# Reading the experts' two sums from GpSimd's queue, adding them on VectorE, and building the matrix of ones ahead of the last expert block

## The chip, the cores and the metric

The kernel runs on one core of one Trainium2 chip. The metric is the device time of one execution in microseconds (us), lower is better; runs are compared by their median.

## The reference, cut to what matters

Two transformer-like blocks follow one another on 512 tokens of 1024 channels. The first ends with a mixture of experts: each token goes to 6 of 64 experts, and a shared expert takes every token.

```
out = lax.map(expert_block, (slot_tok.reshape(n_blocks, MOE_BLOCK), block_exp))
weighted = (out.reshape(n_slots, d) * slot_w[:, None]).astype(h.dtype)
routed = jnp.zeros((t + 1, d), h.dtype).at[slot_tok].add(weighted)[:t]
return (routed + swiglu(hf, s_gate, s_up, s_down)).reshape(bsz, n, d)
...
x = x + gt2 * moe_ffn(...)
return rmsnorm(x, g_final)
```

The second block begins with another norm of that result and a multiplication with `w_in_2`. So the sum over experts has to be complete before the second block can start.

## The kernel before

The experts' work is cut into blocks (`BLOCKS`), each of up to 128 token slots: one expert, or two or four side by side. For each block, `blocks` (L1643) loads the experts' weights into a ring of slots (`load_block`, SyncE's queue), gathers the tokens' rows from DRAM into one of three buffers `Xt` (`gather`, L1588, an indirect DMA on GpSimd's queue), and calls `ffn` (L1598): TensorE turns the rows (`pt_xb`), VectorE and ScalarE scale them in turns into `xTb` (L1343, L1341), TensorE multiplies with gate and up (`gub`), ScalarE and VectorE make `hb` (L1615, L1617), TensorE turns it and multiplies with the down weights (`pyb`), and VectorE scales the result into `yb` (L1631). `scatter` (L1634) then adds the rows of `yb` to one of two buffers in DRAM, `yacc[0]` and `yacc[1]`, in turns, by an indirect DMA with addition on GpSimd's queue. It runs one block late, so the rows of a block are scattered after the next block's `ffn` has been issued.

The last block is not scattered. Ahead of its `ffn` the kernel calls `sums(0)` (L1682), which reads `yacc[0]` into two ring slots with four loads of 512 KB from SyncE's queue, issues the scatter that is still pending, and calls `sums(1)` for `yacc[1]`. GpSimd adds the first sum to `ysh` (L1667), the shared expert's result, four tiles of 128 tokens. After the `ffn` comes `beyond` (L1706): a loop whose count is read at run time (experts with more tokens than planned), on all five engines; its count is zero here. Behind it the second sum is added (L1672, two tiles on VectorE, two on GpSimd), and `combine` (L1689) brings in the last block's rows by TensorE: VectorE builds a matrix of ones from the token numbers (`tfe`, L1695; `ohe`, L1698, comparisons), TensorE multiplies it with `yb` in eight products (`pce`: four token tiles by two halves of the channels), and VectorE adds each from PSUM (L1704).

```
n = nc.values_load(self.nov, min_val=0, max_val=NOV)
with tc.For_i(0, n, 1) as i:
```

The second block (`block_two`, L2237) works on the same tiles, named `x` there. ScalarE squares them (L2278), VectorE multiplies them with g_final (`times`, L2271), ScalarE squares again (L2272), a short chain on VectorE makes the norms (L2282 to L2285), the tiles are scaled (L2288, L2289) and turned by TensorE (`ptn`, L2294 to L2296), and the first products `psi` follow. Their weights are loaded by SyncE (`chunk_w`, L2082) into `wraw`, rounded by ScalarE (`whi`, L273) and completed by VectorE (`wlo`, L274).

Each engine and each DMA queue works through its instructions in a fixed order. The order is not the program's: a scheduler puts it together when the kernel is built, so instructions of two blocks can stand interleaved. No order by hand is set in this part.

Of the kernel before, what the change touches and what calls it, by code (L numbers as in the profile page):

```python
# [7 lines left out]
F32 = mybir.dt.float32  # L8
# [3 lines left out]
ALU = mybir.AluOpType  # L12
# [4 lines left out]
P = 128  # L17
# [267 lines left out]
def stage_norm_in(k, pool, ps, raw):  # L285

    nc, I, V = k.nc, k.I, k.nc.vector
    k.sc = k.pers.tile([P, 8, 32], F32, name="sc")
# [23 lines left out]
    for c in range(8):  # L312
        for i0, n in ((0, 2), (2, 4)):
# [3 lines left out]
            if i0:  # L317
                V.tensor_copy(hx(c), pt)
            else:
# [830 lines left out]
class Moe:  # L1150
# [492 lines left out]
    def blocks(self, bp, ps, hooks, span):  # L1643

        pend, Xs = self.pend, self.Xs
        for n in range(*span):
            b, rows, whos = BLOCKS[n]
            if n == len(BLOCKS) - LEAVE:
                for f in self.first:
                    self.slots.remove(f)  # L1650
            if n == len(BLOCKS) - LAST:

                last = [self.load(w[0]) for _, _, w in BLOCKS[n:]]
                for i in ((0, 1), (2,)):
                    for w in last:
                        for j in i:
                            w[1](j)
            ws = self.load_block(whos)
            self.rows_ahead(min(n + AHEAD, NFIX if span[0] == 0 else len(BLOCKS)))
            if n == len(BLOCKS) - 1:  # L1660

                s0 = self.sums(0)
                while pend:
                    self.scatter(*pend.pop(0))
                s1 = self.sums(1)
                for t in range(4):
                    self.k.nc.gpsimd.tensor_tensor(self.ysh[:, t, :], self.ysh[:, t, :], s0[t], ALU.add)  # L1667
            y = self.ffn(bp, ps, ws, Xs[n], (self.twf if n < NFIX else self.tw)[:, b:b + 1], rows, f"b{b}")
            if n == len(BLOCKS) - 1:
                self.beyond(bp, ps)  # L1670
                for t in range(4):
                    (self.k.nc.gpsimd if t > 1 else self.k.nc.vector).tensor_tensor(self.ysh[:, t, :], self.ysh[:, t, :], s1[t], ALU.add)  # L1672
                self.combine(bp, ps, y, self.tok[:, b:b + 1], rows, "e")
                break
            part = self.parts(n)
            pend.append((y, part))
            if n in hooks:
                hooks[n]()
            while len(pend) > (2 if n < 3 else 1):
                self.scatter(*pend.pop(0))  # L1680

    def sums(self, i):  # L1682

        s = [self.slot(f"sum{i}{j}").rearrange("p (t d) -> p t d", t=2) for j in range(2)]
        for t in range(4):
            self.k.nc.sync.dma_start(s[t // 2][:, t % 2, :], self.yacc[i][t * P:(t + 1) * P])
        return [s[t // 2][:, t % 2, :] for t in range(4)]

    def combine(self, pool, ps, y, tok, n, nm):  # L1689

        nc = self.k.nc
        V = nc.vector
        tf = pool.tile([P, 4], F32, tag="tf", name="tf" + nm, bufs=1)
        for t in range(4):
            V.tensor_scalar(tf[0:n, t:t + 1], tok[0:n], float(-P * t), None, ALU.add)  # L1695
        oh = pool.tile([P, 8, P], F32, tag="xT", name="oh" + nm)
        for t in range(4):
            V.tensor_scalar(oh[0:n, t, :], self.col0[0:n], tf[0:n, t:t + 1], None, ALU.is_equal)  # L1698
        for t in range(4):
            for half in range(2):  # L1700
                cs = slice(512 * half, 512 * half + 512)
                pc = ps.tile([P, 512], F32, tag=("py", "tp", "gu")[(2 * t + half) % 8 // 3], name=f"pc{nm}{t}{half}")
                nc.tensor.matmul(pc, oh[0:n, t, :], y[0:n, cs], start=True, stop=True)
                V.tensor_tensor(self.ysh[:, t, cs], self.ysh[:, t, cs], pc, ALU.add)  # L1704

    def beyond(self, bp, ps):  # L1706
        k, nc, tc = self.k, self.k.nc, self.k.tc
        V = nc.vector
        n = nc.values_load(self.nov, min_val=0, max_val=NOV)
        with tc.For_i(0, n, 1) as i:  # L1710
            sl = bp.tile([P, 1], I32, tag="sl", name="sl_o")
            sw = bp.tile([P, 1], F32, tag="sw", name="sw_o")
            V.tensor_copy(sl, self.tok[:, bass.ds(i + NB, 1)])
            V.tensor_copy(sw, self.tw[:, bass.ds(i + NB, 1)])
            v = nc.sync.value_load(self.eov[:, bass.ds(i, 1)], min_val=0, max_val=NE - 1)
            src = k.I["ew"][bass.ds(v, 1)].rearrange("a p f -> p (a f)")
            ws = []
            for q in range(3):
                t = self.slot(f"ew_o{q}")
                nc.sync.dma_start(t, src[:, 2048 * q:2048 * q + 2048])  # L1720
                ws.append(t)
            X = self.gather(sl)
            y = self.ffn(bp, ps, [ws], X, sw, P, "o")
            self.combine(bp, ps, y, sl, P, "o")

# [782 lines left out]
```

## Time and profile before

| | |
|---|---|
| median of 3 runs | 2020.23 us (2017.06 to 2023.76) |
| the profiled execution, its own time | 2015.22 us |
| its span in the profile | 2013.3 us |
| mean granted clock of TensorE | 0.968 of full speed |

The profile shows the profiled execution alone; times in it count from the start of its span. PE is TensorE's matmul, PEld its weight loads, DVE is VectorE, ACT ScalarE, POOL GpSimd, SP SyncE; a name with a q (SPq) is an engine's queue of instructions that do no arithmetic, DMA issues among them. The granted clock of a stretch is given as a share of full speed.

### The profile page before, as it was taken

How to read it: one execution, taken by the hardware profiler on the slowest of the kernel's cores; microseconds unless marked ns; L12 is line 12 of the kernel's file. 1: busy time of each engine (PE TensorE's matmuls, PEld its weight loads, DVE VectorE, ACT ScalarE, POOL GpSimd, SP SyncE). 2: the span in 40 equal slices, each digit the busy share in tenths (PEclk: the TensorE clock that was granted, in tenths of full speed). 3: DMA queues.
4: the chain of work that ended last, by engine and by line, in shares of the span. 5: the costliest groups of instructions: out<-in, count | busy, mean ns of one | idle time of the engine just before them, and what ended most of it. 6: DMA issues, size and time to landing. Idle time of an engine off the chain costs nothing.

```text
span 2013.3 us, 24229 instructions
## 1 busy us (share of the span) xinstructions
PE 1826.9 (91%) x8481; PEld 1237.6 (61%) x8481; DVE 993.3 (49%) x2220; ACT 596.5 (30%) x1124; POOL 502.1 (25%) x407
## 2 busy tenths in 40 slices
PE   5897778996879999989999987999999999999998
PEld 3686556885644333333333335888888788888886
DVE  4689955668776222262222227776423453323352
ACT  5453311213423111111111114433423344323341
POOL 1314343442422222212212225342001113101300
PEclk9998988998989999999999998999999999999999
DMA  8354353226488998999999983332323423233241
GB/s 313 118 179 161 88 163 99 80 60 214 151 299 300 355 369 346 350 398 380 367 366 370 375 321 127 111 106 79 115 89 92 143 85 105 89 94 100 79 141 42
DMA packets 135555, 393.64 MB, mean 196 GB/s; under 512 B 46899, under 2 KB 59443, under 8 KB 109064
## 3 DMA queue, kind: packets, MB, share of 16 engines
q1 hardware_dynamic: 109752, 363.66, 50.7%
q0 software_dynamic: 11856, 26.83, 5.3%
q10 hardware_dynamic: 13824, 1.58, 0.5%
q8 instruction: 68, 1.11, 0.2%
q14 instruction: 55, 0.45, 0.1%
HBM read 365.19 MB, written 38.54 MB: 201 GB/s over the span
## 4 chain that ended last, share of the span: by engine, by line
PE 69%; DVE 15%; DMA 10%; ACT 3%; issue 2%; POOL 1%; SPq 0%; another core or an unknown queue 0%; ACTq 0%; POOLq 0%; DVEq 0%
PE psi L139 12%; PE gub L139 10%; PE pof L139 9%; PE psf L139 9%; PE pyb L139 6%; DMA ewrank<-ew 6%; PE psco L139 2%; DVE cfa L746 2%; PE poo L139 2%; DVE gt L569 1%; PE pxca L139 1%; PE pt_xb L142 1%; PE pm L139 1%; PE psga L139 1%; PE psgb L139 1%
## 5 line engine op out<-in xcount | busy, mean ns | idle before, releaser
L139 PE MATMUL gub<-ewrank,xTb 128*64 128x512 f32 (+5 forms) x960 | 266.6, 596 | 1.2 <-DMA ewrank<-ew 0.6
L274 DVE TENSOR_TENSOR wlo<-wraw,whi 128x1024 fp32r<-128x1024 f32 (+1 forms) x103 | 121.7, 1182 | 137.7 <-ACT whi L273 136.9
L139 PEld LDWEIGHTS gub<-ewrank,xTb 128*64 128x64 f32 (+5 forms) x960 | 90.0, 141 | 158.3 <-issue 144.1
L273 ACT CAST whi<-wraw 128x1024 fp32r<-128x1024 f32 (+1 forms) x115 | 113.8, 989 | 226.5 <-PE psi L139 50.6
L139 PE MATMUL pyb<-ewrank,hTb 128*64 128x512 f32 (+5 forms) x440 | 152.4, 607 | 3.4 <-DMA ewrank<-ew 1.4
L139 PE MATMUL psi<-xnh,whi 128*128 128x512 f32 (+1 forms) x368 | 141.2, 385 | 0.0
L139 PE MATMUL psi<-xnl,whi 128*128 128x512 f32 (+1 forms) x368 | 140.9, 383 | 0.0
L1617 DVE SCALAR_TENSOR_TENSOR hb<-gub,tw,sgb 128x256 f32<-128x256 f32 (+5 forms) x38 | 18.3, 482 | 230.3 <-ACT sgb L1615 230.3
L1639 POOL DMA_INDIRECT yacc<-yb,tok x61 | 86.1, 1411 | 158.3 <-DVE yb L1631 109.3
L1341 ACT ACTIVATE xTb<-pt_xb,B,A 128x128 f32<-128x128 f32 (+5 forms) x168 | 74.0, 445 | 173.2 <-DVE xTb L1343 171.8
L139 PE MATMUL psi<-xnh,wlo 128*128 128x512 f32 (+1 forms) x296 | 112.8, 381 | 0.0
L1593 POOL DMA_INDIRECT X<-hrow,tok x38 | 39.6, 1042 | 291.2 <-PE pt_xb L142 285.9
L1343 DVE TENSOR_SCALAR xTb<-pt_xb,A,B 128x128 f32<-128x128 f32 (+5 forms) x168 | 65.5, 392 | 88.2 <-PE pt_xb L142 51.9
L2433 POOL TENSOR_TENSOR fr<-fr 128x512 f32<-128x512 f32 x32 | 48.6, 1518 | 238.2 <-ACT fr L2432 238.2
L139 PE MATMUL psf<-xml,whi 128*128 128x512 f32 (+1 forms) x272 | 102.6, 377 | 0.2 <-DVE xml L274 0.2
L139 PE MATMUL psf<-xmh,whi 128*128 128x512 f32 (+1 forms) x272 | 102.5, 378 | 0.2 <-ACT xmh L273 0.2
L139 PE MATMUL psf<-xmh,wlo 128*128 128x512 f32 (+1 forms) x272 | 102.5, 377 | 0.0
L1631 DVE TENSOR_TENSOR yb<-pyb,gt 128x512 f32<-128x512 f32 (+5 forms) x84 | 57.9, 690 | 72.0 <-PE pyb L139 70.5
L1615 ACT ACTIVATE sgb<-gub 128x256 f32<-128x256 f32 (+5 forms) x42 | 16.0, 382 | 260.3 <-PE gub L139 260.3
L139 PEld LDWEIGHTS pyb<-ewrank,hTb 128*64 128x64 f32 (+5 forms) x440 | 46.4, 142 | 74.9 <-issue 63.7
L139 PEld LDWEIGHTS psi<-xnh,whi 128*128 128x128 f32 x368 | 69.2, 189 | 13.8 <-issue 0.2
L139 PEld LDWEIGHTS psi<-xnl,whi 128*128 128x128 f32 x368 | 69.2, 188 | 13.4
(755 smaller groups left out, 4030.1 us busy)
## 6 DMA issues: line engine op xcount, KB each, us to landing
ewrank<-ew SPq DMA_DIRECT2D x168, 1024.0 KB, 25.1
wraw<-w_in SPq DMA_DIRECT2D x59, 512.0 KB, 3.7
wraw<-ff SPq DMA_DIRECT2D x32, 512.0 KB, 3.5
wf<-ff SPq DMA_DIRECT2D x64, 256.0 KB, 2.7
wm<-w_mod SPq DMA_DIRECT2D x28, 512.0 KB, 7.8
ewfix<-ew SPq DMA_DIRECT2D x12, 1024.0 KB, 16.9
ewx<-ew SPq DMA_DIRECT2D x12, 1024.0 KB, 19.6
wm<-w_mod SPq DMA_DIRECT2D x10, 1024.0 KB, 6.2
```

What stands on the lines that cost most here:

```text
L139: return self._done(self.eng.matmul(out, lhsT, rhs, **kw), rate, rhs)
L142: return self._done(self.eng.transpose(out, in_, ident), 0.00118, ident)
L273: nc.scalar.copy(hi, raw)
L274: (eng or nc.vector).tensor_tensor(lo, raw, hi.bitcast(F32), ALU.subtract)
L569: eng.tensor_tensor(t, S[0:nq, w:32, b:w].to_broadcast([nq, n, b]), S[0:nq, b:w, 0:b].to_broadcast([nq, n, b]), ALU.mult)
L746: V.scalar_tensor_tensor(a[:, r0 * 64:r1 * 64], y[:, (r0 + o) * 64:(r1 + o) * 64], w[:, j, 15 + o:16 + o], a[:, r0 * 64:r1 * 64], ALU.mult ...
L1341: nc.scalar.activation(dst(c), pt[:, i, :], AF.Identity, scale=sa, bias=sb)
L1343: nc.vector.tensor_scalar(dst(c), pt[:, i, :], sa, sb, ALU.mult, ALU.add)
L1593: self.k.nc.gpsimd.indirect_dma_start(out=X[0:idx.shape[0]], out_offset=None, in_=self.hrow, in_offset=bass.IndirectOffsetOnAxis(ap=idx, a ...
L1631: nc.vector.tensor_tensor(y[0:n, cs], py[0:n], self.gt2[0:n, cs], ALU.mult)
L1639: self.k.nc.gpsimd.indirect_dma_start(out=self.yacc[1 - self.nsc % 2], out_offset=bass.IndirectOffsetOnAxis(ap=idx, axis=0), in_=y[a:a + n ...
L2433: nc.gpsimd.tensor_tensor(r, r, r, ALU.mult)
```

## The change

The two reads of `sums` move from SyncE's to GpSimd's queue, and each reads half of the tokens (256 rows, 1 MB) in one load. The first sum is added by VectorE and no longer by GpSimd. `combine` is split: `ones_at` builds the matrix of ones, for the last block ahead of its `ffn`, in the gather buffer `Xt[1]`, and `combine` does the eight products, now ordered so that the first two token tiles come first, half by half. The adds of the second sum (L1672) stay as they are. In `beyond`, whose loop isn't entered, the same functions are called.

```diff
                 s1 = self.sums(1)
                 for t in range(4):
-                    self.k.nc.gpsimd.tensor_tensor(self.ysh[:, t, :], self.ysh[:, t, :], s0[t], ALU.add)
+                    self.k.nc.vector.tensor_tensor(self.ysh[:, t, :], self.ysh[:, t, :], s0[t], ALU.add)
+                oh = self.ones_at(bp, self.tok[:, b:b + 1], rows, "e")
             y = self.ffn(bp, ps, ws, Xs[n], (self.twf if n < NFIX else self.tw)[:, b:b + 1], rows, f"b{b}")
...
-                self.combine(bp, ps, y, self.tok[:, b:b + 1], rows, "e")
+                self.combine(ps, y, oh, rows, "e")
                 break
...
         s = [self.slot(f"sum{i}{j}").rearrange("p (t d) -> p t d", t=2) for j in range(2)]
-        for t in range(4):
-            self.k.nc.sync.dma_start(s[t // 2][:, t % 2, :], self.yacc[i][t * P:(t + 1) * P])
+        for j in range(2):
+            self.k.nc.gpsimd.dma_start(s[j], self.yacc[i][256 * j:256 * j + 256].rearrange("(t p) d -> p t d", p=P))
         return [s[t // 2][:, t % 2, :] for t in range(4)]
 
-    def combine(self, pool, ps, y, tok, n, nm):
-
-        nc = self.k.nc
-        V = nc.vector
+    def ones_at(self, pool, tok, n, nm):
+
+        V = self.k.nc.vector
         tf = pool.tile([P, 4], F32, tag="tf", name="tf" + nm, bufs=1)
         for t in range(4):
             V.tensor_scalar(tf[0:n, t:t + 1], tok[0:n], float(-P * t), None, ALU.add)
-        oh = pool.tile([P, 8, P], F32, tag="xT", name="oh" + nm)
+
+        oh = self.Xt[1][:, 0:4 * P].rearrange("p (t a) -> p t a", t=4)
         for t in range(4):
             V.tensor_scalar(oh[0:n, t, :], self.col0[0:n], tf[0:n, t:t + 1], None, ALU.is_equal)
-        for t in range(4):
-            for half in range(2):
-                cs = slice(512 * half, 512 * half + 512)
-                pc = ps.tile([P, 512], F32, tag=("py", "tp", "gu")[(2 * t + half) % 8 // 3], name=f"pc{nm}{t}{half}")
-                nc.tensor.matmul(pc, oh[0:n, t, :], y[0:n, cs], start=True, stop=True)
-                V.tensor_tensor(self.ysh[:, t, cs], self.ysh[:, t, cs], pc, ALU.add)
+        return oh
+
+    def combine(self, ps, y, oh, n, nm):
+
+        nc = self.k.nc
+        for i, (t, half) in enumerate([(t + u, half) for t in (0, 2) for half in range(2) for u in range(2)]):
+            cs = slice(512 * half, 512 * half + 512)
+            pc = ps.tile([P, 512], F32, tag=("py", "tp", "gu")[i // 3], name=f"pc{nm}{t}{half}")
+            nc.tensor.matmul(pc, oh[0:n, t, :], y[0:n, cs], start=True, stop=True)
+            nc.vector.tensor_tensor(self.ysh[:, t, cs], self.ysh[:, t, cs], pc, ALU.add)
...
-            self.combine(bp, ps, y, sl, P, "o")
+            self.combine(ps, y, self.ones_at(bp, sl, P, "o"), P, "o")
```

## Rows read from the trace of the kernel before

**Rows 1.** The head of the page: the span and the engines' busy time.

```profile
span 2013.3 us, 24229 instructions
...
PE 1826.9 (91%) x8481; PEld 1237.6 (61%) x8481; DVE 993.3 (49%) x2220; ACT 596.5 (30%) x1124; POOL 502.1 (25%) x407
```

**Rows 2.** Table by stretches: PE, PEld, DVE, ACT, POOL busy, clock, DMA share, GB/s.

```profile
1204.00:1214.00 10.00, 5.44 (x26) 1.66 (x20) 1.87 (x3) 0.76 (x2) 9.22 (x4) 1.00 0.43 139
1214.00:1224.00 10.00, 8.83 (x16) 3.56 (x16) 8.64 (x16) 2.27 (x3) 4.79 (x5) 0.83 0.57 210
```

**Rows 3.** Timeline of POOL from 1190 us: start, duration, instruction [idle before, releaser].

```profile
1198.85 1.42 POOL L1639 DMA_INDIRECT yacc<-yb,tok  x1 [11.10 <-DVE yb L1631]
1204.78 9.26 POOL L1667 TENSOR_TENSOR h<-h,sum 128x1024 f32<-128x1024 f32 x4 [4.51 <-DMA sum<-yacc]
1218.35 4.68 POOL L1672 TENSOR_TENSOR h<-h,sum 128x1024 f32<-128x1024 f32 x2 [4.31 <-DVE h L1704]
```

**Rows 4.** SP's queue at the sums: timelines, and one of its waits (total, times, longest).

```profile
1194.63 0.81 SPq L1686 DMA_DIRECT2D sum<-yacc  x2
...
1206.31 0.80 SPq L1686 DMA_DIRECT2D sum<-yacc  x2
...
1214.28 0.80 SPq L1686 DMA_DIRECT2D sum<-yacc  x2
...
SPq L1710 <- DMA yacc<-yb,tok: 4.7, 1, 4.7
```

**Rows 5.** The chain that ended last, two of its pieces: start, us, what.

```profile
1186.33 8.25 DMA yacc<-yb,tok
...
1215.13 5.71 DMA wraw<-w_in
```

**Rows 6.** Timeline of DVE from 1190 to 1230 us.

```profile
1195.22 0.41 DVE L1343 TENSOR_SCALAR xTb<-pt_xb,A,B 128x128 f32<-128x128 f32 x1 [0.59 <-ACT xTb L1341]
1196.17 0.69 DVE L1631 TENSOR_TENSOR yb<-pyb,gt 80x512 f32<-80x512 f32 x1 [0.54 <-PE pyb L139]
...
1199.42 0.41 DVE L1343 TENSOR_SCALAR xTb<-pt_xb,A,B 128x128 f32<-128x128 f32 x1 [0.53 <-ACT xTb L1341]
1205.85 0.48 DVE L1617 SCALAR_TENSOR_TENSOR hb<-gub,tw,sgb 128x256 f32<-128x256 f32 x1 [6.03 <-ACT sgb L1615]
...
1211.09 0.69 DVE L1631 TENSOR_TENSOR yb<-pyb,gt 128x512 f32<-128x512 f32 x1 [0.21 <-PE pyb L139]
1214.37 0.34 DVE L1695 TENSOR_SCALAR tfe<-tok 128x1 f32<-128x1 int32 x4 [2.59 <-POOL h L1667]
1214.62 0.67 DVE L1698 TENSOR_SCALAR ohe<-col,tfe 128x128 f32<-128x128 f32 x3
1215.20 1.22 DVE L1672 TENSOR_TENSOR h<-h,sum 128x1024 f32<-128x1024 f32 x1
...
1221.94 2.17 DVE L274 TENSOR_TENSOR wlo<-wraw,whi 128x1024 fp32r<-128x1024 f32 x1
...
1225.83 2.35 DVE L2271 TENSOR_TENSOR h<-h,row_g_final 128x1024 f32<-128x1024 f32 x2
...
1228.17 1.21 DVE L274 TENSOR_TENSOR wlo<-wraw,whi 128x1024 fp32r<-128x1024 f32 x1
```

**Rows 7.** Timeline of TensorE's matmuls from 1185 to 1234 us.

```profile
1185.38 7.03 PE L139 MATMUL gub<-ewrank,xTb 128*80 128x512 f32 x16
...
1214.95 8.83 PE L139 MATMUL pce<-yb,ohe 128*128 128x512 f32 x16 [3.90 <-DVE ohe L1698]
1233.47 0.90 PE L142 MATMUL ptn<-cst,sums 128*128 128x128 f32 x3 [9.69 <-ACT sums L2288]
```

**Rows 8.** POOL's and SP's direct loads of 512 KB elsewhere (us to landing), POOL's time for two.

```profile
inv<-o POOLq DMA_DIRECT2D x2, 512.0 KB, 3.9
...
wraw<-w_in SPq DMA_DIRECT2D x59, 512.0 KB, 3.7
...
L580 POOL DMA_DIRECT2D inv<-o x2: 552/728/905, 269.3 to 270.4; - x2
```

## The prediction

> **What bounds the kernel now.** I read the page's head first [rows 1]: TensorE is busy for 91% of a span of 2013.3 us, so only what lets TensorE stand still can be won or lost. The change touches one seam, the end of the experts and the start of the second block, so I read only that: the table by stretches, then each queue between 1186 and 1236 us, then the chain of waits. From 1204 to 1214 us TensorE is busy for 5.44 of 10 us; in the next 10 us it is busy for 8.83, but at a mean granted clock of 0.83 [rows 2]. POOL shows why the seam starts late: its four adds of the first sum begin at 1204.78 us and take 9.26 us, to 1214.04, and the first instruction behind the loop of `beyond` (L1710) is DVE's at 1214.37, released by POOL [rows 3, 6]. Call the loop's exit E: 1214.04 now. DVE's last work ahead of it ends at 1211.78 (the last yb), so POOL holds all engines for over two microseconds. Behind E, DVE is the chain: from 1214.37 to 1225.83 it is full almost without a gap (indices, ones, two adds of sums, eight adds of products, one wlo), then come the multiplications with g_final, and TensorE's next block begins only with ptn at 1233.47, after 9.69 us of idling [rows 6, 7]. What moves ptn moves the end one for one, as TensorE is the bound behind it [rows 1].
>
> **The change part by part.** The sum is made against the profiled execution, 2015.22 us (span 2013.3); the median of the runs is 2020.23, 5.0 above it, so I add the same microseconds to the median.
>
> *The first sum's adds go from POOL to DVE.* POOL needs 9.26 / 4 = 2.3 us for one, DVE 1.22 us for the same shape [rows 3, 6]; four are 4.9 us. Without POOL's 9.26 the loop waits for the next latest: DVE's 1211.78, or SP's own wait at the loop, 4.7 us after its issue at 1206.31 to 1207.1, so about 1211.9 [rows 4, 6]. I put E at 1212.3: 1.7 us saved. The adds are not free on DVE. Their data were there at 1204.78, 10 us after the first issue at 1194.63 [rows 3, 4]. DVE idles from 1199.83 to hb at 1205.85 and from there to about 1210.2 (1211.09 less 0.21 and the 0.69 of the yb before), but only the second gap lies behind the landing, and 3.9 us of it holds three adds of four. The fourth, or one ahead of hb, costs up to 1.2 us; I take 0.6. Bounds for this term: nothing, and 3.7 us (all four ahead of hb, the first rival). Net so far: 1.1 us saved.
>
> *The reads go from SP's queue to POOL's, two of 1 MB for four of 512 KB.* POOL's direct loads of 512 KB land after 3.9 us, SP's after 3.7, and hold POOL for 0.73 us each [rows 8]; I take twice that, 1.5 us, for 1 MB, bounds 0.7 and 1.5. Ahead of the first sum POOL waits for the scatter issued at 1186.33, landed 8.25 us later, at 1194.57 [rows 5]; its two reads then occupy it to about 1197.6, and the next scatter, held until then by yb, starts at 1198.85 [rows 3]. So that scatter covers for them; without that cover they would cost up to 3 us. The second sum waits on POOL's queue for that scatter instead of on SP's; behind the waiting instruction stands only the loop, where POOL must arrive by 1212. From 1206.3 plus 2 x 1.5 us it does. Cost 0. SP loses its two reads behind the loop, which stood ahead of the weight load at 1215.13 [rows 4, 5]: 0.85 us earlier for a load that took 5.71 us. That load ends in whi and then wlo at 1221.94; DVE had other work until then, so alone it is worth nothing, but it keeps the load from becoming late when DVE's chain shrinks.
>
> *The ones are built ahead of the last ffn, in a gather buffer that the block before it read.* That removes four index adds (0.34 us) and four comparisons (0.67 for three, so 0.22 for the fourth) from DVE behind E [rows 6]. In place, 1214.37 to 1215.20 and the fourth are 1.05 us of DVE's chain; I take 1.1 saved (bounds 0.6, the advance of the first product, at E + 0.9 now and at E + 0.3 then [rows 7]; and 1.25). Their new place is DVE's idle time before hb; if that is gone they cost the same 1.25 us there.
>
> *The products' order* (two tokens' tiles, half by half) keeps the first four products on the same two tiles and the same eight PSUM tiles. Nothing waits on one tile's second half alone before all eight adds; cost 0, bounds 0.7 us either way (one add).
>
> *What else shifts.* The wlo at 1221.94 took 2.17 us, while POOL's second pair of adds ran to 1223.03; the next of its shape took 1.21 [rows 3, 6]. If the second sum lands earlier POOL's pair and the wlo no longer meet: bounds 0 and 0.96, I take 0.5. The clock: TensorE idles 3.9 us ahead of the first product, and the products take 8.83 us at 0.83 clock; at the full clock the block before did 16 in 7.03 [rows 2, 7]. With a shorter gap the clock may stay up: bounds 0 and 1.8; I take 0, since the gap remains.
>
> **Sum**: 1.1 + 1.1 + 0.5 = 2.7 us saved, 0.13%: 2015.22 becomes 2012.5, and the median 2020.23 becomes 2017.5.
>
> **A rule weighed.** POOL's scatter at 1198.85 took 1.42 us with DVE's xTb at 1199.42 beside it [rows 3, 6]; a row in which a DVE add of two SBUF operands stands beside POOL's descriptors is not there. The Trainium skill (SBUF — State Buffer, SBUF: two separate sides, the box on the "DVE blocks DMA" trap) says that a DMA issued from GpSimd waits while DVE runs a two-port instruction, and advises the SP or ACT queue, the opposite of this change; the same page (Who interferes with whom) infers that a tensor_tensor takes only the read side. By the box, the sum would lose two of DVE's adds, 2.4 us, and be 0.3; by the row it stays 2.7. I keep the row; the other case is the fifth rival.
>
> **Rivals.**
> 1. *hb waits behind all four adds.* The order on DVE is fixed before the run and not by the program: two xTb of the last block (1195.22) ran ahead of the yb of the block before it (1196.17) [rows 6]. If the adds are ordered into the gap 1199.83 to 1205.85, they wait for 1204.7 and end at 1209.6: hb is 3.7 us late, E is 1211.78 + 3.7 + 0.3 = 1215.8, 1.7 later than now; 1.1 and 0.5 come back: 2020.3. For it: the gap is the widest. Against: POOL's adds were ordered behind the scatter at 1198.85, so the order expects the sums late. Chance 0.26.
> 2. *Slower: the adds stand ahead of the last block's second pair of xTb* (the later at 1199.42). Then DVE stops until 1209.6, the pair is 10 us late, the gate products too, and E is 1211.78 + 10.3 + 0.3, about 1222.4 to 1223: 8.4 to 9 later; less 1.6, some +7.2, 2027.4. It decides from the first add that stands ahead of 1199.42 in DVE's order. Against it: in POOL's order the adds came after a scatter at 1198.85, and reads of 1 MB are ready no earlier than reads of 512 KB. Chance 0.14.
> 3. *E doesn't move*: both halves of the second sum are now issued ahead of the loop, and it waits for their landing: 1206.3 + 3.0 of issue + about 5 is 1214. Then the change does not do the first of its savings: 1.1 + 0.5, 2018.6. Chance 0.12.
> 4. *The clock stays up* and everything meets: 1.7 + 1.1 + 0.96 + 1.8 = 5.6, 2014.6. Chance 0.08.
> 5. *DVE's adds hold up POOL's reads behind E* by two adds, 2.4 us: 2017.5 + 2.4 = 2019.9. Chance 0.05; the scatter of [rows 3] speaks against it. It is what the box of the Trainium skill (SBUF — State Buffer, above) would make of this place.
>
> **How the numbers follow.** My forecast has 0.35, the rivals 0.65. A measurement of this kernel tells about 0.3%, 6 us, from no change; the three runs alone lie 6.7 us apart. All cases but the second lie within 6 us of 2020.23. The runs' spread (3 us to each side) carries a third of case 4 and a quarter or so of the forecast and of terms I have sized too small beyond 6 us: faster 0.18. Case 2, with its own spread, gives slower 0.13. The rest, 0.69, is no change. The range goes from case 4 less some of the spread, 2012, to just short of case 2, 2026; about 0.1 lies above and less below.
>
> **What would show it.** Right: no POOL adds between 1204 and E; the first instruction behind the loop near 1212.5; products starting within 0.4 us of it, no is_equal on DVE behind it; ptn 2 to 4 us earlier. The four DVE adds behind xTb at 1199.42 confirm that rival 2 is out; hb later than 1206 by up to 3.7 is rival 1. Wrong: E unmoved, or hb of the last block later than 1210, or ptn moved while the end does not.

## The result, and the profile after

The change makes the kernel slower: 2031.68 us median of 6 runs (2027.67 to 2033.42) against 2019.38 of 6 runs of the kernel before (2017.06 to 2023.76), a ratio of 1.006 with a 95% interval of 1.0048 to 1.0073. That is 12.3 us more, outside the range of 2012 to 2026. The profiled execution took 2029.28 us with a span of 2027.3, which is 14.0 above the span of before [rows 1].

In what follows the times of the seam are counted from the start of the last block's gub products (1198.21 us in the trace before, 1197.39 in the trace after), since what lies ahead of them shifts a few microseconds from run to run. "Exit" is the start of the first pce product, the first matmul behind the loop; it stands at +16.7 before and at +28.2 after.

The head of the page of the kernel after:

```profile
span 2027.3 us, 24232 instructions
...
PE 1833.0 (90%) x8481; PEld 1239.5 (61%) x8481; DVE 998.5 (49%) x2224; ACT 596.3 (29%) x1124; POOL 498.5 (25%) x407
```

The table by stretches, with the columns of [rows 2]:

```profile
1197.00:1204.00 7.00, 2.33 (x13) 0.71 (x11) 0.00 (x0) 0.00 (x0) 0.00 (x0) 0.95 0.80 330
1204.00:1214.00 10.00, 5.49 (x14) 1.44 (x16) 6.97 (x9) 1.37 (x3) 1.54 (x1) 0.52 0.27 64
1214.00:1224.00 10.00, 6.65 (x30) 2.07 (x26) 2.88 (x4) 1.74 (x3) 1.48 (x2) 1.00 0.59 212
1224.00:1234.00 10.00, 7.13 (x16) 2.96 (x16) 8.28 (x7) 1.11 (x2) 5.71 (x4) 1.00 0.29 105
1234.00:1244.00 10.00, 0.00 (x0) 0.00 (x0) 9.69 (x27) 7.48 (x14) 0.00 (x0) 0.67 0.22 70
...
1249.00:1254.00 5.00, 3.64 (x18) 3.34 (x17) 4.72 (x13) 2.10 (x6) 3.35 (x2) 0.50 0.00 0
```

Two things are new. From 1197 to 1204 us DVE, ACT and POOL do nothing at all, and TensorE is busy for 2.33 of 7 us. And TensorE has about half of its clock while it has work to do: 0.52 from 1204 to 1214, where the kernel before had 1.00 [rows 2], and 0.50 from 1249 to 1254, from 4 to 9 us behind the start of ptn. The clock of the kernel before fell around ptn too, but mostly while TensorE idled, and it was full again 3.5 us behind ptn's start (1233.47):

```profile
1224.00:1234.00 10.00, 0.53 (x3) 0.53 (x4) 9.55 (x26) 8.44 (x15) 1.12 (x1) 0.61 0.50 157
...
1237.00:1242.00 5.00, 4.54 (x37) 4.37 (x38) 4.69 (x21) 2.27 (x6) 3.46 (x2) 1.00 0.36 107
```

DVE's timeline says what everyone waits for (it answers to [rows 6]):

```profile
1193.41 0.41 DVE L1343 TENSOR_SCALAR xTb<-pt_xb,A,B 128x128 f32<-128x128 f32 x1 [0.89 <-PE pt_xb L142]
1205.01 2.36 DVE L1667 TENSOR_TENSOR h<-h,sum 128x1024 f32<-128x1024 f32 x2 [11.19 <-DMA sum<-yacc]
1207.28 0.68 DVE L1631 TENSOR_TENSOR yb<-pyb,gt 80x512 f32<-80x512 f32 x1
1207.89 0.40 DVE L1343 TENSOR_SCALAR xTb<-pt_xb,A,B 128x128 f32<-128x128 f32 x1
1208.20 0.68 DVE L1631 TENSOR_TENSOR yb<-pyb,gt 80x512 f32<-80x512 f32 x1
1209.45 2.36 DVE L1667 TENSOR_TENSOR h<-h,sum 128x1024 f32<-128x1024 f32 x2 [0.57 <-DMA sum<-yacc]
1211.73 0.41 DVE L1343 TENSOR_SCALAR xTb<-pt_xb,A,B 128x128 f32<-128x128 f32 x1
1212.66 0.41 DVE L1343 TENSOR_SCALAR xTb<-pt_xb,A,B 128x128 f32<-128x128 f32 x1 [0.53 <-ACT xTb L1341]
1217.06 0.48 DVE L1617 SCALAR_TENSOR_TENSOR hb<-gub,tw,sgb 128x256 f32<-128x256 f32 x1 [3.99 <-ACT sgb L1615]
...
1222.90 1.22 DVE L274 TENSOR_TENSOR wlo<-wraw,whi 128x1024 fp32r<-128x1024 f32 x1
1225.84 6.27 DVE L1673 TENSOR_TENSOR h<-h,sum 128x1024 f32<-128x1024 f32 x2 [1.72 <-issue]
1232.03 4.86 DVE L1709 TENSOR_TENSOR h<-h,pce 128x512 f32<-128x512 f32 x8
```

The first sum's adds (L1667) stand in DVE's order ahead of the yb of the block *before* the last one and ahead of three of the four xTb that DVE makes for the last block. They wait 11.19 us for the reads. Everything behind them waits too: hb comes at +19.7 (before: +7.6), and the late yb holds the last scatter on POOL, which answers to [rows 3]:

```profile
1194.27 1.61 POOL L1687 DMA_DIRECT2D sum<-yacc  x2 [7.34 <-DMA ewrank<-ew]
1209.17 1.54 POOL L1639 DMA_INDIRECT yacc<-yb,tok  x1 [13.29 <-DMA wraw<-w_in]
1215.99 1.48 POOL L1687 DMA_DIRECT2D sum<-yacc  x2 [5.27 <-PE gub L139]
1225.39 5.63 POOL L1673 TENSOR_TENSOR h<-h,sum 128x1024 f32<-128x1024 f32 x2 [7.93 <-issue]
```

The scatter goes out at 1209.17 instead of 1198.85 (its row names a weight load, but yb ends at 1208.88, just ahead of it, and in the run e10 below the same row names yb). It lands 5.0 us later, and the second sum, which needs its rows, is read from 1215.99, 1.8 us behind the landing (that row names gub; in e1, where gub is long over, the reads start 1.8 us behind the landing too). Both of its halves now stand ahead of the loop, and SP's waits (total, times, longest) show the loop (L1715) waiting for the scatter first and then for those reads:

```profile
SPq L1715 <- DMA yacc<-yb,tok: 23.9, 1, 23.9
...
SPq L1715 <- DMA sum<-yacc: 5.7, 1, 5.7
```

That last wait ends at 1224.3. DVE's last instruction ahead of the loop, the wlo behind the late yb, ends at 1224.12: two delays reach the loop at the same time.

TensorE's timeline, which answers to [rows 7], has the bill:

```profile
1197.39 1.94 PE L139 MATMUL gub<-ewrank,xTb 128*64 128x512 f32 x8
1208.34 3.68 PE L139 MATMUL gub<-ewrank,xTb 128*64 128x512 f32 x8 [9.01 <-DVE xTb L1343]
1212.19 4.32 PE L139 MATMUL gub<-ewrank,xTb 128*64 128x512 f32 x16 [0.17 <-DVE xTb L1343]
...
1225.59 7.13 PE L139 MATMUL pce<-yb,X 128*128 128x512 f32 x16 [3.33 <-issue]
1245.05 2.96 PE L142 MATMUL ptn<-cst,sums 128*128 128x128 f32 x12 [12.33 <-ACT sums L2293]
```

Added up, span against span: gub starts 0.8 us earlier; from there to hb 19.67 us instead of 7.64, **+12.0** (9.01 and 0.17 of idling, and 9.94 us for the 32 gub products where the kernel before has 7.09, as the clock had fallen); hb to exit 8.53 instead of 9.10, −0.6; exit to ptn 19.46 instead of 18.52, +0.9; ptn to the end 782.3 instead of 779.8, +2.4, with the half clock of 1249 to 1254 in it. Together 14.0. It looks as if one wait on DVE explained the result. The experiments show that undoing it alone gives back about a third.

### The profile page after: what moved, and what is told of

It reads as the page before. It is cut to its first block, busy times and chain, and to the rows that moved or that the text cites. A ratio compares the mean times of both kernels' runs of the same rounds, so it can differ in the third digit from the quotient of the medians.

```text
span 2027.3 us, 24232 instructions
## 1 busy us (share of the span) xinstructions
PE 1833.0 (90%) x8481; PEld 1239.5 (61%) x8481; DVE 998.5 (49%) x2224; ACT 596.3 (29%) x1124; POOL 498.5 (25%) x407
## 5 line engine op out<-in xcount | busy, mean ns | idle before, releaser
L1617 DVE SCALAR_TENSOR_TENSOR hb<-gub,tw,sgb 128x256 f32<-128x256 f32 (+5 forms) x38 | 18.3, 482 | 227.7 <-ACT sgb L1615 227.7
```

The source lines that it names most:

```text
L1617: nc.vector.scalar_tensor_tensor(h[0:n], gu[0:n, 256:512], wslot[0:n], sg[0:n], ALU.mult, ALU.mult)
```

## The experiments

Fourteen kernels, in the order of the argument. The table gives the ratio to the kernel before with its 95% interval and the places of hb, exit and ptn behind the start of the last gub, in us, from one trace of each kernel.

The medians of the kernel before beside them were 2018.71 to 2019.84 us.

| kernel | ratio (interval) | hb | exit | ptn |
|---|---|---|---|---|
| before | 1 | 7.6 | 16.7 | 35.3 |
| after | 1.0060 (1.0048 to 1.0073) | 19.7 | 28.2 | 47.7 |
| e1 after, adds behind hb | 1.0042 (1.0029 to 1.0054) | 7.6 | 25.3 | 44.7 |
| e2 before, adds on DVE | 1.0013 (1.0002 to 1.0024) | 7.6 | 20.1 | 39.1 |
| e3 before, reads on POOL | 1.0100 (1.0086 to 1.0115) | 7.6 | 39.4 | 57.8 |
| e4 after, reads on SP | 1.0012 (1.0000 to 1.0023) | 7.6 | 18.3 | 37.3 |
| e5 before, ones and order | 0.9999 (0.9987 to 1.0010) | 7.6 | 16.7 | 36.3 |
| e6 after, first sum on SP | 1.0029 (1.0018 to 1.0040) | 7.6 | 20.1 | 41.8 |
| e7 e1, second sum on SP | 1.0048 (1.0030 to 1.0066) | 7.6 | 21.2 | 41.8 |
| e8 e6, all second adds on DVE | 1.0035 (1.0022 to 1.0047) | 7.6 | 20.3 | 38.8 |
| e9 e1, second sum behind the loop | 1.0043 (1.0024 to 1.0062) | 7.6 | 17.3 | 43.2 |
| e10 after, all second adds on DVE | 1.0048 (1.0030 to 1.0066) | 19.0 | 28.4 | 45.8 |
| e11 e4, adds pinned behind hb | 1.0009 (0.9997 to 1.0021) | 7.6 | 18.3 | 37.0 |
| e12 e11, all second adds on DVE | 1.0011 (1.0002 to 1.0021) | 7.6 | 18.3 | 38.4 |
| e13 e4, adds between hb and yb | 1.0004 (0.9994 to 1.0015) | 7.6 | 16.2 | 35.6 |
| e14 e13, two of them on POOL | 1.0007 (0.9997 to 1.0018) | 7.6 | 15.9 | 35.2 |

**e1: the order alone.** The changed kernel, with an order (no wait) that puts the first sum's adds behind the last block's hb.

```diff
-                for t in range(4):
-                    self.k.nc.vector.tensor_tensor(self.ysh[:, t, :], self.ysh[:, t, :], s0[t], ALU.add)
...
+            if n == len(BLOCKS) - 1:
+                for t in range(4):
+                    q = self.k.nc.vector.tensor_tensor(self.ysh[:, t, :], self.ysh[:, t, :], s0[t], ALU.add)
+                    self.k.tc.add_manual_dep(q.ins, self.mark["h"].ins.name, ...)
```

> The changed kernel whole, but VectorE's four adds of the first sum are ordered behind hb of the last block (order alone, the same engine). Theory A (order): the loss comes from the two pairs of adds that stand ahead of yb and of the last block's second pair of xTb and wait for reads that land at 1205.0 and 1209.4 us. Then gub of the last block runs without a stop again (from about 1197.4 to 1204.6), hb comes near 1205, the loop's exit near 1214 to 1216 instead of 1225.4, and of the 12 us lost some 9 to 11 come back: ratio to before 1.000 to 1.002. Rival B (queue): the loss is that of the reads on GpSimd's queue, which hold the scatter and land late; then the adds wait all the same, behind hb, the exit stays past 1220 and the ratio stays at 1.004 or above.

2027.94 us. The order is repaired entirely (gub unbroken in 7.09 us, hb at +7.6), yet of the 12.3 us only about 3.6 come back (1.0060 to 1.0042; the two intervals overlap, so the size is uncertain), where 9 to 11 were expected. The exit moves from +28.2 to +25.3 alone, and ptn by 3.0 us. POOL's timeline of this run has the rest:

```profile
1196.65 1.61 POOL L1690 DMA_DIRECT2D sum<-yacc  x2 [7.43 <-DMA yacc<-yb,tok]
1200.33 1.54 POOL L1640 DMA_INDIRECT yacc<-yb,tok  x1 [2.07 <-DVE yb L1632]
1215.24 1.48 POOL L1690 DMA_DIRECT2D sum<-yacc  x2 [13.37 <-issue]
1224.72 5.62 POOL L1676 TENSOR_TENSOR h<-h,sum 128x1024 f32<-128x1024 f32 x2 [8.00 <-issue]
```

The scatter is on time again, but the reads that need its rows go out 14.9 us behind it (1215.24 less 1200.33), where the kernel before had 7.5 (1198.85 to 1206.31, [rows 3, 4]). Most of that is the scatter's own way: from its issue to its landing it takes 13.1 us here and 7.4 in the kernel before. After it the loop waits for the reads. So there were two delays side by side in the changed kernel, of nearly the same length: hb late through the order, and the second sum late. To take away one of them gives back only the difference.

**e2 to e5: each part of the change alone.** e2 is the kernel before with the first sum's adds on DVE; e3 the kernel before with the reads on POOL's queue, in two loads of 1 MB; e4 the changed kernel with the reads back on SP's; e5 the kernel before with the ones built early and the products by halves.

```diff
 e2
-                    self.k.nc.gpsimd.tensor_tensor(self.ysh[:, t, :], self.ysh[:, t, :], s0[t], ALU.add)
+                    self.k.nc.vector.tensor_tensor(self.ysh[:, t, :], self.ysh[:, t, :], s0[t], ALU.add)
 e3 (e4 is the reverse, on the changed kernel)
-        for t in range(4):
-            self.k.nc.sync.dma_start(s[t // 2][:, t % 2, :], self.yacc[i][t * P:(t + 1) * P])
+        for j in range(2):
+            self.k.nc.gpsimd.dma_start(s[j], self.yacc[i][256 * j:256 * j + 256].rearrange("(t p) d -> p t d", p=P))
 e5 (on the changed kernel: reads as before, and)
-                    self.k.nc.vector.tensor_tensor(self.ysh[:, t, :], self.ysh[:, t, :], s0[t], ALU.add)
+                    self.k.nc.gpsimd.tensor_tensor(self.ysh[:, t, :], self.ysh[:, t, :], s0[t], ALU.add)
```

> The kernel before with one edit: the first sum's four adds go from GpSimd to VectorE; reads, ones and products stay. Theory A: VectorE's adds harm only where they are ordered ahead of xTb and yb; here they stand behind the first yb of the last block, so nothing waits for them but the loop: 4 x 1.2 us behind 1211 plus some 1.6 us of the loop's own semaphores on VectorE, exit near 1217 to 1218, ptn 3 to 4 us later, ratio 1.001 to 1.002. If the adds on VectorE were the loss by themselves wherever they stand (rival), the ratio would be 1.005 or above; if GpSimd's adds were all that held the exit, as the forecast had it, 0.999 to 1.000.

> The kernel before with one edit: the two sums are read by GpSimd's queue in two loads of 1 MB; the adds stay on GpSimd, the ones stay late. Theory A (the reads on GpSimd's queue make the order expect the sums early): three of GpSimd's four adds now stand ahead of the last scatter, which waits for them: scatter at some 1212 instead of 1198.85, the second sum's reads at some 1219, exit near 1221 to 1223, ratio 1.003 to 1.005, though no add is on VectorE. Rival C (the adds on VectorE are the cause): nothing on VectorE waits, ratio 0.999 to 1.001.

> The changed kernel whole with one part undone: the reads are four of 512 KB on SyncE's queue again. VectorE's adds then stand at the last block's yb and behind. Theory A: gub of the last block runs without a stop, exit near 1217 to 1218 as in the kernel with VectorE's adds alone, the ones' 1 us is gained behind it: ratio 1.0005 to 1.002. Rival (adds on VectorE): 1.005 or above.

> The kernel before with two edits alone: the matrix of ones built ahead of the last ffn, and the products ordered by halves of the tokens; reads on SyncE's queue and the first sum's adds on GpSimd as before. From the start of the last block's gub, the kernel before reaches the loop's exit after 16.0 us and ptn after 35.3. Theory A (the loss is in the reads and the adds): the exit stays, ptn comes 0.6 to 1.1 us earlier for the ones: ratio 0.9993 to 1.000. Rival (the early ones on VectorE, or their place in the gather buffer, hold something): ptn later, ratio above 1.001.

The medians are 2022.27, 2040.94, 2022.26 and 2019.14 us. The reads carry the loss: by themselves they cost 1.0%, 20 us, more than the whole change, and the change without them costs 0.12% (e4), which is what the adds on DVE cost alone (e2). The ones and the products' order give nothing that can be measured (e5). The loss of e3 is more than twice what was expected of it.

e3 shows also that the way the sums are read sets where the built order puts the adds. In the kernel before POOL's four adds stood behind the scatter [rows 3]; with the reads on POOL's queue, in two loads in place of four, and nothing else changed, three stand ahead of it:

```profile
1199.38 1.58 POOL L1686 DMA_DIRECT2D sum<-yacc  x2 [7.42 <-DMA yacc<-yb,tok]
1210.33 6.96 POOL L1667 TENSOR_TENSOR h<-h,sum 128x1024 f32<-128x1024 f32 x3 [9.36 <-DMA sum<-yacc]
1217.46 2.33 POOL L1639 DMA_INDIRECT yacc<-yb,tok  x1 [0.17 <-issue]
1219.26 2.90 POOL L1667 TENSOR_TENSOR h<-h,sum 128x1024 f32<-128x1024 f32 x1
1225.25 1.50 POOL L1686 DMA_DIRECT2D sum<-yacc  x2 [3.09 <-issue]
```

On DVE the same holds: with SP's reads (e2, e4) the first add follows the last block's first yb, at +12.6; with POOL's (after) it stands behind the first xTb, ahead of everything else of that block. The queue and the size of the loads change together in every run here; which of the two tips the order is not shown.

**e6, e7: one sum on each queue.** e6 reads the first sum from SP's queue and the second from POOL's; e7 is e1 (adds behind hb) the other way round.

```diff
+        if (0, 1)[i]:      # e7: (1, 0)
             for j in range(2):
                 self.k.nc.gpsimd.dma_start(...)
+        else:
+            for t in range(4):
+                self.k.nc.sync.dma_start(s[t // 2][:, t % 2, :], self.yacc[i][t * P:(t + 1) * P])
```

> The changed kernel, but the first sum is read by SyncE's queue again and only the second by GpSimd's. Theory D (one queue: in the changed kernel the last scatter stands behind the first sum's reads on GpSimd's queue and lands only after them): here no read stands ahead of the scatter, it lands some 7 us after its issue as before, the second sum's reads go out about 9 us after the start of gub and land by 18; exit after 17.5 to 19 us, ratio 1.000 to 1.0015. Rival E (any large read on GpSimd's queue is slow, or delays the loop): exit after 23 us or more, ratio 1.003 or above.

> The kernel with the adds behind hb, but the second sum is read by SyncE's queue (four of 512 KB) and only the first by GpSimd's. Theory D (one queue): the last scatter still stands behind the first sum's reads and lands 14 to 15 us after its issue, so SyncE's reads of the second sum go out no earlier than 15 us after the start of gub; exit after 21 to 25 us, ratio 1.003 to 1.005. Rival E: with only half of the traffic on GpSimd's queue, half of that loss is back, exit after 18 to 20 us, ratio 1.001 to 1.002.

2025.07 and 2028.16 us; e6 loses more than was expected of it. In e6 no read stands ahead of the scatter on POOL's queue: it lands after 7.6 us, and the second sum's reads go out 8.2 us behind it (+0.6 to +8.8). In e7 the first sum's reads do stand ahead of it, and it takes 10.6 us (+0.7 to +11.3): longer than 7.6, but less than e1's 13.1 and less than was expected. The scatter's time from issue to landing in the kernel before, in e7 and in e1, the last number of each row:

```profile
yacc<-yb,tok POOLq DMA_INDIRECT x1, 7.4
yacc<-yb,tok POOLq DMA_INDIRECT x1, 10.6
yacc<-yb,tok POOLq DMA_INDIRECT x1, 13.1
```

In both e1 and e7 the scatter lands only behind the reads issued ahead of it on that queue: the second read at +12.3 and the scatter at +13.8 in e1, +9.7 and +11.3 in e7. The load of the DMA engines does not explain it: from +4 to +8 us their busy share was 0.82 in e6 and only 0.58 in e7 and 0.62 in e1. That the queue works them off in order is what this suggests. Why the first sum's reads themselves landed later in e1 than in e7 stays open; one difference that the traces show is that in e1 SP had sent two weight loads of the second block by then, and in e7 it sent none before +20.6.

e6 has the scatter free, and still loses 0.29%. Its loop waits for both halves of the second sum (exit +20.1, against +18.3 in e4), and then DVE's two adds take 6.67 us beside POOL's two of 5.64.

**e9: is it the loop that waits?** e1 with the second sum's reads written behind the loop, into two tiles of the ring that the loop itself fills, so that they can't be ordered ahead of it.

```diff
-                s1 = self.sums(1)
...
                 self.beyond(bp, ps)
+                self.slots[:0] = [self.slots.pop(), self.slots.pop()]
+                s1 = self.sums(1)
```

> The changed kernel with the first sum's adds behind hb (as in e1) and the second sum's two reads issued from POOL's queue only behind the loop. Times are counted from the start of the last block's gub. Theory (the loop's exit waits for whatever reads were issued ahead of it to land): the exit falls from +25 to +18..+20, set by the last scatter, which still stands behind the first sum's reads and lands near +15; the reads then go out at about +19 and land near +28, so that the second sum's adds and ptn are hardly earlier than in e1 (ptn +43..+46, e1 +44.7) and the ratio stays at 1.003 to 1.0045: the same landing is waited for behind the exit instead of ahead of it. Rival (the exit at +25 is due to DVE's or POOL's own work and not to the reads): the exit stays at +25 and ptn comes 8 us later than in e1.

2027.29 us. The exit falls from +25.3 to +17.3, 8 us, by this alone: the loop did wait for the reads to land. And nothing is won, as expected: the data are as late as ever, and now the adds wait for them. POOL's timeline behind the loop, and one row of DVE's:

```profile
1218.72 1.49 POOL L1691 DMA_DIRECT2D sum<-yacc  x2 [16.74 <-issue]
1229.15 4.65 POOL L1677 TENSOR_TENSOR h<-h,sum 128x1024 f32<-128x1024 f32 x2 [8.94 <-DMA sum<-yacc]
```
```profile
1225.34 2.36 DVE L1677 TENSOR_TENSOR h<-h,sum 128x1024 f32<-128x1024 f32 x2 [5.82 <-DMA sum<-yacc]
```

ptn comes at +43.2 (e1: +44.7). Here POOL's pair and DVE's do not meet in time, and each takes what it takes alone: 4.65 and 2.36 us.

**e8, e10: the second sum's adds, all on DVE.** e8 is e6, e10 the changed kernel, each with

```diff
-                    (self.k.nc.gpsimd if t > 1 else self.k.nc.vector).tensor_tensor(self.ysh[:, t, :], self.ysh[:, t, :], s1[t], ALU.add)
+                    self.k.nc.vector.tensor_tensor(self.ysh[:, t, :], self.ysh[:, t, :], s1[t], ALU.add)
```

> As the kernel with only the second sum on GpSimd's queue, but all four adds of the second sum are VectorE's (two were GpSimd's). In the changed kernel VectorE's pair took 6.27 us beside GpSimd's pair, 2.4 us alone. Theory F (the two engines hold each other up when both add in SBUF): VectorE's four adds take 4.9 us, GpSimd none; what comes behind them is 1 to 2 us earlier than with the pairs side by side: ratio to before 0.999 to 1.001, 0.0005 to 0.001 below its twin. Rival (they do not hold each other up, the long pair waits for data): VectorE's two more adds cost 2.4 us, ratio 0.001 above its twin.

> The changed kernel with all four adds of the second sum on DVE (POOL has none). Theory (DVE's pair of 6.27 us is stretched by POOL's pair beside it): the four adds take 4.6 to 5.0 us together on DVE, ptn comes 2.5 to 3.5 us sooner behind the exit (after: 19.5 us from pce's start to ptn, here 16.5), ratio 1.0040 to 1.0055. Rival (the stretch is something else, or DVE waits for another thing next): the two adds of the first half still take over 5 us, or ptn stays at 19 us or more behind pce's start; ratio 1.006.

2024.95 and 2029.44 us. DVE's row of e10:

```profile
1225.48 4.63 DVE L1673 TENSOR_TENSOR h<-h,sum 128x1024 f32<-128x1024 f32 x4 [2.18 <-issue]
```

Four adds take 4.63 us where two beside POOL's pair took 6.27. Behind the exit ptn comes 2.0 us sooner in e10 than after (17.5 against 19.5; I had expected 2.5 to 3.5) and 3.2 sooner in e8 than in e6 (18.5 against 21.7). The ratios can't confirm a gain of this size: 1.0048 against 1.0060 for e10, 1.0035 against 1.0029 for e8, with intervals that overlap; e8 was expected at 0.999 to 1.001 and missed. So the stretching is shown, its worth in the total is not.

**e11 to e14: the step on the first sum's adds, by itself.** All have the reads on SP's queue. e11 pins the adds behind hb as e1 does, e12 has the second sum's adds on DVE as well; e13 holds yb behind the adds too, so that they stand where the prediction put them; e14 leaves two of the four on POOL.

```diff
 e13 (in ffn, for the last block)
+        for t in range(4 if s0 else 0):
+            q = self.k.nc.vector.tensor_tensor(self.ysh[:, t, :], self.ysh[:, t, :], s0[t], ALU.add)
+            if t < 4:
+                self.k.tc.add_manual_dep(q.ins, hop.ins.name, ...)
+                dve.append(q)
...
+            for q in dve:
+                self.k.tc.add_manual_dep(yop.ins, q.ins.name, ...)
 e14
+            q = (self.k.nc.gpsimd if t > 1 else self.k.nc.vector).tensor_tensor(self.ysh[:, t, :], self.ysh[:, t, :], s0[t], ALU.add)
+            if t < 2:
```

> The change with the reads back on SP's queue and the first sum's four adds on DVE pinned behind hb of the last block, where the prediction put them. Theory (the prediction's step of the four adds holds by itself, only its place and the reads failed): the adds fill the gap between hb (+7.6) and yb, 4.9 us; yb ends at +14.2..+14.6 and the exit (pce's start) is at +16.0..+16.7 (before: +16.7); ptn +34.5..+36; ratio 0.9990 to 1.0003. Rival (DVE's adds stretch beside PE's or the DMA's work, or yb goes late behind them): yb ends over +15, the exit at +17.5 or later as in e4 (+18.3), ratio 1.0010 to 1.0015.

> As e11, and the second sum's four adds on DVE as well. Theory (POOL's pair, 4.68 us from the landing of the second half to its end, sets the last products' adds in the kernel before; DVE's pair takes 2.4 us): the last pce add ends some 2 us sooner behind the exit than in e11 and ptn stands at +32.5..+34; ratio 0.9980 to 0.9995, the best of all. Rival (the order puts DVE's adds of the late half ahead of products' adds whose data are there, so that DVE waits for the landing and gives the 2 us back): ptn +35 or later, ratio 0.9995 to 1.0005.

> The change with the reads back on SP's queue, the first sum's four adds on DVE between hb and yb of the last block, and yb held behind them. Times from the start of the last block's gub. Theory (the step holds by itself): adds from +8.0 to +12.7, yb ends at +14.1, pce's start (exit) at +14.6..+15.5 (before: +16.7); ptn +33.5..+35 (before +35.3); ratio 0.9992 to 1.0000. Rival (the step fails by itself: the exit waits for the second sum's reads, of which three go out ahead of the loop here and two in the kernel before): pce at +16.5..+19, ptn +35..+38, ratio 1.0000 to 1.0012.

> As e13, but two of the four adds (the second half of the tokens) stay on POOL. Theory: DVE's two go from +8.0 to +10.4, POOL's two from about +6.6 to +11.5, yb ends at +13.6 as in the kernel before, the exit is set by yb: pce at +14.0..+15; ptn +32.7..+34.5; ratio 0.9985 to 0.9998, the best of all kernels. Rival (the exit waits for the landing of the second sum's first half, issued at about +8 and landed near +12, and for the loop's own semaphores): pce at +16..+17 as before, ratio 0.9998 to 1.0008.

2020.69, 2021.59, 2019.40 and 2019.24 us. e11 and e12 missed: "behind hb" is a lower bound only, and the adds were ordered at yb as in e4 (first add at +12.6, exit +18.3). With the second adds on DVE too, ptn is no earlier (+38.4 against +37.0).

In e13 the adds do stand in the gap, 4.68 us from +8.0 without a pause, and yb ends 0.35 us later than before:

```profile
1204.95 4.68 DVE L1622 TENSOR_TENSOR h<-h,sum 128x1024 f32<-128x1024 f32 x4
1209.56 1.28 DVE L1639 TENSOR_TENSOR yb<-pyb,gt 128x512 f32<-128x512 f32 x2
1212.99 4.51 DVE L1682 TENSOR_TENSOR h<-h,sum 128x1024 f32<-128x1024 f32 x2 [2.16 <-DMA sum<-yacc]
```

But the exit comes only 0.6 us earlier (+16.2). Three of the second sum's four reads were ordered ahead of the loop here, which waits for them (DVE's 2.16 us of idling, released by DMA sum<-yacc), and then the two pairs of adds meet again: 4.51 us on DVE, 6.47 on POOL. In e14 the loop waits for POOL's two adds of the first sum, which have their data later than DVE's:

```profile
1208.96 4.78 POOL L1622 TENSOR_TENSOR h<-h,sum 128x1024 f32<-128x1024 f32 x2 [8.07 <-DMA sum<-yacc]
1218.13 4.68 POOL L1682 TENSOR_TENSOR h<-h,sum 128x1024 f32<-128x1024 f32 x2 [4.38 <-DMA sum<-yacc]
```

Its exit is 0.8 us earlier than before and its ptn 0.1. Both exits are later than expected (+14.6 to +15.5 and +14.0 to +15), and neither ratio differs from 1. No kernel of this study beats the kernel before by an amount that can be measured.

## Why the prediction was wrong, step by step

**The step that failed is the second: "The reads go from SP's queue to POOL's ... Cost 0."** It priced two things, the time that issuing takes on POOL (1.5 us for a load, so 3.0 for two; measured are 1.61 and 1.48 for two) and whether the scatter covers it (in e1 it goes out at +0.65, in the kernel before at +0.64). The first was twice too much, the second right, and neither matters. The reads are worth 1.0060 less 1.0012, some 10 us of the 12.3 (after against e4). Three mechanisms were not in that price, two of them put among the rivals; each is shown by a run:

- *The place of the adds in the built order.* Rival 2 described it, with 0.14, and its argument against, "reads of 1 MB are ready no earlier than reads of 512 KB", was about the chip: there it holds (10.7 us from issue to the first add, 10.1 before, [rows 3, 4]). But the order is made ahead of the run, and with nothing changed but the queue and the size of the reads it put three POOL adds ahead of the scatter (e3) and DVE's adds behind the first xTb (after). What it reckons with the traces don't show; that the reads tip it they do. To undo it in the changed kernel is worth some 3.6 us (e1). Rival 2 is what happened, and its price, 2027.4, was 4.3 us short: it had no term for the clock that falls while TensorE waits, 2.85 us in the gub products alone (9.94 less 7.09).
- *The scatter behind the reads on one queue.* "So that scatter covers for them" looked at POOL's instructions, not at the transfers. The next thing needed is the scatter's landing, and with reads ahead of it on the queue that takes 10.6 us (e7) to 13.1 (e1) instead of 7.4. In the changed kernel this delay was hidden, since the late yb kept the scatter back until the reads had all but landed (5.0 us then).
- *The loop waits for reads issued ahead of it.* Rival 3 had the mechanism (chance 0.12) and sized it with "about 5" us of landing and the reads at 1206.3: E unmoved. The reads went out at 1215.99 and SP's wait for them is the last one ahead of the loop; e9 shows 8 us of exit that hang on it. The landing of 1 MB took longer too: DVE's pair in e9 starts 6.6 us, POOL's 10.4 us after the issue began.

The step's gain for SP, a weight load "0.85 us earlier", was misread too: with the sums' reads gone from SP's queue, the first two weight loads of the second block went out at 1182.64 and 1185.42 instead of from 1215.13, beside the first sum's reads.

**The first step, adds from POOL to DVE, 1.1 us saved.** Where the order put the adds (e2, e4) it costs 0.12 to 0.13%, with an exit 1.6 to 3.4 us later; where the step wanted them (e13) the exit gains 0.6 us instead of 1.7, and ptn nothing. The durations were right (4.68 us for four, 4.9 predicted). Wrong was E at 1212.3, half a microsecond behind DVE's 1211.78: where DVE is the last engine to reach the loop, its first instruction behind it starts 1.72 us after its last one ahead of it (the idle time of L1673's first add in e4 and of L1676's in e11), so that the yb allows about 1213.5; and the second sum's reads, ordered ahead of the loop, are waited for.

**The third step, ones early, 1.1 us saved: measured nothing** (e5: 0.9999, exit +16.7, ptn +36.3 against +35.3). DVE's chain is not the only one there. Its timeline in e5 shows who takes the place:

```profile
1220.29 2.36 DVE L1673 TENSOR_TENSOR h<-h,sum 128x1024 f32<-128x1024 f32 x2 [3.03 <-POOL h L1667]
1222.57 2.47 DVE L1709 TENSOR_TENSOR h<-h,pce 128x512 f32<-128x512 f32 x4
1226.47 0.69 DVE L1709 TENSOR_TENSOR h<-h,pce 128x512 f32<-128x512 f32 x1 [1.42 <-POOL h L1673]
1228.78 0.69 DVE L1709 TENSOR_TENSOR h<-h,pce 128x512 f32<-128x512 f32 x1 [1.63 <-POOL h L1673]
```

DVE now waits 1.42 and 1.63 us for POOL's pair, which starts at +20.4 as it did at +20.1. The timeline of before showed DVE full [rows 6], and the text took full for critical.

**The wlo beside POOL's pair, 0.5 us saved.** The contention was seen in the right place and looked for in the wrong instruction. The wlo went ahead of the loop (1.22 us); DVE's own pair of adds met POOL's, now that both halves land together: 6.27 instead of 2.36 us, and POOL's 5.63 instead of 4.65 (e9). The Trainium skill (SBUF — State Buffer, Who interferes with whom) says that a DVE instruction with two SBUF inputs contends with a GpSimd instruction that reads SBUF. These rows agree with it: the rule that mattered stood beside the one that was weighed.

**Rival 5, the box on "DVE blocks DMA".** In the changed kernel POOL's scatter at 1209.17 has a DVE add of two SBUF operands beside it, but the add begins 0.28 us behind the scatter. The scatter takes 1.54 us, as in e1 and e7, where no such add is near: nothing was held up, and the reads were late for other reasons. One row of the runs has the other order, in e3, where a DVE instruction with two SBUF operands is already running when the scatter at 1217.46 begins:

```profile
1215.91 2.47 DVE L274 TENSOR_TENSOR wlo<-wraw,whi 128x1024 fp32r<-128x1024 f32 x1
```

The wlo runs 0.92 us into that scatter, which takes 2.33 us; the 975 other scatters of this kind in the sixteen traces take 1.3 to 1.6. The box of the Trainium skill (SBUF — State Buffer, SBUF: two separate sides) says that a DMA issued from GpSimd waits while DVE runs an instruction in a two-port mode. The row looks like such a wait behind a tensor_tensor, which the inference that the prediction weighed does not allow for. It is one row, worth under 1 us, and the changed kernel has none like it.

**The signs that were named.** "hb of the last block later than 1210" came true (1217.06). "The four DVE adds behind xTb at 1199.42 confirm that rival 2 is out" was badly put: the adds began behind that time, at 1205.01, and stood ahead of that xTb in the order. An order can't be read from a time of the other trace.

## What to carry to other kernels

Here the move of two reads to another engine's queue moved three things besides their issue: the transfer behind them on that queue landed later (13.1 us instead of 7.4 in e1), the built order of the adds that use them changed, and a loop waited for them. So price the landing of the next transfer on the queue, not the time of its issue; and find out what each engine's order is before pricing the work on it. Where two delays lie side by side, undoing one shows only the difference, so each part has to be tried both alone and taken out.

## What the runs showed that was not expected

- Adds of two SBUF operands on DVE and POOL at the same time: where POOL's pair began first (after, e1, e6) DVE's took 6.27 to 6.67 us instead of 2.36, POOL's 5.62 to 5.64 instead of 4.65; in e13, where DVE's pair began 0.27 us sooner, 4.51 and 6.47. Two adds beside POOL cost DVE more than all four alone (4.63, e10).
- Read under the load of the weights (DMA share 0.83 from 1180 to 1204 us), the two 1 MB reads from POOL's queue are 10.7 and about 14 us under way (after: issued from 1194.27, used at 1205.01 and 1209.45).
- The half clock follows the idling. In the changed kernel TensorE stood still for 9.01 us ahead of the second gub group and had a granted clock of 0.52 over the stretch from 1204 to 1214 us, near the lower of its two levels (1.2 of 2.4 GHz); it stood still for 12.33 us ahead of ptn, and had 0.50 from 1249 to 1254. The kernel before had no gap ahead of that gub group and 9.69 us ahead of ptn [rows 7], and its clock was full again 3.5 us behind ptn's start. So the end did not move one for one with ptn, as the prediction had it: the part behind ptn grew by 2.4 us.
